# Layer 0's experts: the residual streams return from DRAM before the last pair's outputs, which one-hot products add on the chip

## The chip, the cores and the metric

One core of a Trainium2 chip runs the whole program. Its engines have a queue of instructions each: PE (TensorE matmuls, with PEld for the weight loads), DVE (VectorE), ACT (ScalarE), POOL (GpSimd) and SP (SyncE, which here only starts DMAs). The metric is the device time in microseconds (us). Three runs of the kernel before took 2985.73, 2987.39 and 2992.25 us.

## The reference

Two blocks of two layers each run one after the other on one stream of 512 tokens by 1024 features. The change lies in the first layer of the second block, which carries a second stream, a context of 256 tokens. At the end of that layer each stream gets the outputs of 16 experts, each expert picking its own tokens:

```python
def _expert_choice_ffn(h, w_router, w_gate, w_up, w_down):
    b, t, d = h.shape
    cap = EC_CAPACITY_FACTOR * t // N_EXPERTS          # 64 latent tokens, 32 context tokens
    aff = jax.nn.softmax(jnp.einsum('btd,de->bte', h, w_router).astype(jnp.float32), axis=-1)
    vals, idx = lax.top_k(aff.transpose(0, 2, 1), cap)
    xg = jax.vmap(lambda hb, ib: hb[ib])(h, idx)
    hid = jax.nn.silu(jnp.einsum('becd,edf->becf', xg, w_gate)) * jnp.einsum('becd,edf->becf', xg, w_up)
    out = jnp.einsum('becf,efd->becd', hid, w_down) * vals[..., None].astype(h.dtype)
    return jax.vmap(lambda ob, ib: jnp.zeros((t, d), h.dtype).at[ib.reshape(-1)].add(ob.reshape(-1, d)))(out, idx)

# in the layer:   x  = x  + m_lat[5] * _expert_choice_ffn(h2, ...)      (latent, 512 tokens)
#                 cx = cx + m_ctx[5] * _expert_choice_ffn(hc2, ...)     (context, 256 tokens)
# the next layer: h = rmsnorm(x) * ..., hc = rmsnorm(cx) * ...  and products with w_in
```

`rmsnorm` divides each token by the root of the mean of its 1024 squares. Everything is f32.

## The kernel before, in words

**The streams.** On the chip `x` (latent) and `cx` (context) lie with the features on the 128 partitions, as 8 slices of [128, tokens]. The router writes a copy with one token per row to DRAM, `acc`, and the experts' outputs are added there: row `r` of a tile `row` is added to the row of `acc` that an index names (`scatter`, L1811, an indirect DMA on POOL's queue that adds). After the last expert `reload` fetches `acc` back in six loads of 128 tokens (tile `in`, issued from ACT's queue, L1822), squares each token's row and sums it (ACT, L1824), turns it by 8 PE transposes (L1828) into PSUM, and DVE copies these into `x` and `cx` (L1830).

**The experts.** They are taken in eight pairs q = 0 to 7. For a pair, `gu` is the gate and up product: context experts on 32-column tiles of PE into PSUM tile `pso` (L1756), latent ones on 64-column tiles into `psg` (L1764). Four products with 32 columns, or two with 64, run side by side on PE; such a group is called a round below. Four transposes per stream turn the hidden rows (`hid`, L1738). `d` is the down product: context into `psa` (L1777), then latent in two halves of 512 features into `pss` (L1791). DVE scales each by the router's value and the layer's gate into `row` (L1783, L1794), and two scatters per stream add it to `acc`. The list `acts` in `ffn` sets the order: gu0, gu1, d0, gu2, d1, and so on to gu7, d6, d7.

**The weights** come in 96 pieces of 1 MB over SP's queue in the order of `acts`, into a ring of 14 slots: 11 of tile `ew` and 3 spare ones, which are the memory of `x` and `cx` themselves, since the streams are in DRAM meanwhile. The last pair's down product therefore still reads weights out of `x` (the rows `pss<-x,hid`).

**The scheduler** orders each engine's queue from its estimate of when inputs are there, so operations that are written one after the other in the code can be interleaved. PSUM has tags `g` (two tiles), `o`, `a`, `s` and `t`; a new tile waits until the readers of the old one are done.

**After the experts** the next layer's mixer norms both streams: the root from the sums (`rsqrt`, some ten DVE operations on a few columns, L309 to L325), one row of it over all partitions (`row_of`, L414 and L416), `norm_steps` (L439 to L449), and PE products with `w_in` whose weights are fetched and split by `load` (`wr`, `wh`, `wl`, L458 to L462; products L472 to L474). Where sums of squares are taken elsewhere in the kernel, PE multiplies the squares with a column of ones (L402).

Of the kernel before, what the change touches and what calls it, by code (L numbers as in the profile page):

```python
# [90 lines left out]
def _layout(inp):  # L91
# [16 lines left out]
    _layout2(g, A, vec2, c2)  # L108
    c2["id"] = np.eye(P, dtype=np.float32)
    A["const1"], coff = _pack(c)  # L110
    A["const2"], coff2 = _pack(c2)
# [123 lines left out]
class _K:  # L235
# [1324 lines left out]
    def route(self, l, v, x, nt, cap, state, got):  # L1560
# [61 lines left out]
        for r in range(ne):  # L1622
            o = pg[r * cap:(r + 1) * cap]
            ten.matmul(o[:, :ng], fi, one[:, r:16:ne], start=True, stop=False)
            ten.matmul(o[:, 8:16], val, one[:, r % 2:16:2], start=False, stop=r > 0)
            if r == 0:
                ten.matmul(o[:, 16:32], fi, one[:, :16], start=False, stop=True)
# [4 lines left out]
        vw = self.s1(f"vw{v}", [P, 8])  # L1632
        vec.tensor_copy(vw, pg[:, 8:16])
        yield

# [9 lines left out]
    def ffn(self, l, x, cx, need, states):  # L1645
        nc, A = self.nc, self.A
        ten, vec, act = nc.tensor, nc.vector, nc.scalar
        acts = [("gu", 0)] + [a for q in range(1, 8) for a in (("gu", q), ("d", q - 1))] + [("d", 7)]
        pieces = []
        for what, q in acts:  # L1650
# [9 lines left out]
        def fetch():  # L1660
            n = len(loaded) % (EW + len(spare))
            raw = self.tl("ew", [P, 4, 512]) if n < EW else spare[n - EW]
            nc.sync.dma_start(raw, pieces[len(loaded)].rearrange("p (k c) -> p k c", k=4))
            loaded.append(raw)
# [14 lines left out]
        for _ in range(6):  # L1679
            for r in run:  # L1680
                next(r, None)
        self.experts(l, acts, got, eload)
        if need:
            self.reload(x, cx)

# [20 lines left out]

    def experts(self, l, acts, got, eload):

# [3 lines left out]
        self.mods = {v: self.mod_cols(l, v, 3, self.v(f"n2{l}")) for v in got}  # L1712
        two = 1 in got
        rows, xg, hid = {}, {}, {}
# [53 lines left out]
        def down(q):  # L1768
            w = [[eload() for _ in range(2)] for _ in range(2)]
            if two:  # L1770
# [9 lines left out]
                for j in range(2):  # L1780
                    r = slice(j * 64, j * 64 + 64)
                    c = slice(j * 512, (j + 1) * 512)
                    vec.scalar_tensor_tensor(y[:64, c], ps[r], val[r, q:q + 1], gate[r, c], OP.mult, OP.mult)  # L1783
                self.scatter(1, y, si, q, 32)
            gi, si, val, gate = got[0]
            y = self.tl("row", [P, D])
            for j in range(2):
# [6 lines left out]
                vec.scalar_tensor_tensor(y[:, c], ps, val[:, q:q + 1], gate[:, c], OP.mult, OP.mult)  # L1794
            self.scatter(0, y, si, q, 64)

        fetch(0)
        fetch(1)
        inputs(0)
        for what, q in acts:  # L1800
            if what == "gu":
                fetch(q + 2)
                inputs(q + 1)
                gate_up(q)
            else:
                down(q)

# [7 lines left out]
    def reload(self, x, cx):  # L1815

        nc = self.nc
        ss = self.s1("ssr", [P, 6])
        for v, xs, nt, c0 in ((1, cx, 2, 0), (0, x, 4, 2)):
            for i in range(nt):  # L1820
                row = self.tl("in", [P, D])
                nc.scalar.dma_start(row, self.acc[v][i * P:(i + 1) * P, :])  # L1822
                j = self.tl("row", [P, D])
                nc.scalar.activation(j, row, AF.Square, accum_out=ss[:, c0 + i:c0 + i + 1])  # L1824
                for s in range(2):
                    pq = self.pt("t")
                    for k in range(4):
                        nc.tensor.transpose(pq[:, k * P:(k + 1) * P], row[:, (4 * s + k) * P:(4 * s + k + 1) * P], self.idf)  # L1828
                    d = xs[:, 4 * s:4 * s + 4, i * P:(i + 1) * P]
                    nc.vector.tensor_copy(d, pq.rearrange("p (k c) -> p k c", k=4))  # L1830
            c = slice(c0, c0 + nt)
            self.rsqrt(ss[:, c], nt, 1.0 / D, self.rs2[:, c])

# [58 lines left out]
```

## Time and profile before

| | |
|---|---|
| median of three runs | 2987.39 us (2985.73 to 2992.25) |
| the profiled execution | 2988.55 us, of which 2986.7 us are the span from the first to the last instruction |
| PE busy | 2787.1 us (93%) |
| DVE, ACT, POOL busy | 1544.5 us (52%), 1195.2 us (40%), 279.0 us (9%) |
| mean granted TensorE clock | 0.971 of 2.4 GHz |
| the experts of layer 0 whose order changes (gu7, d6, d7) | 2201.8 to 2253.3 us |
| return of the streams, to the latent root's start | 2253.3 to 2281.3 us |

A share of busy time is a mean over stages; what the change touches is the stretch of some 80 us from 2201.8 us on, some 3% of the span. There the rows further down are read: the windows give the busy time of each engine in a stretch, and the timeline gives the start and length of each instruction and what ended the idle time before it.

### The profile page before, as it was taken

The page shows a single profiled execution, that of the slowest core. Times are in us where ns is not written, and L with a number is a line of the kernel's source. Part 1 is how long each engine was busy: PE and PEld are TensorE (multiplying, and loading weights), DVE is VectorE, ACT ScalarE, POOL GpSimd, SP SyncE. Part 2 cuts the span into 40 slices and gives each one's busy share as a digit, 9 for nine tenths or more (in the row PEclk, how much of TensorE's full clock was granted, in tenths as well). Part 3 has the DMA queues.
Part 4 walks back from the last instruction along what each step waited for, and adds up shares of the span by engine and source line. Part 5 has one row for each costly group of instructions (what it writes and reads, how often), then busy time and mean ns, then how long its engine had stood idle before and what let it go on. Part 6 is the DMA issues. An engine that isn't in the chain of part 4 may idle for free. (4 is left out here: it accounts for less than half of the span.)

```text
span 2986.7 us, 46938 instructions
## 1 busy us (share of the span) xinstructions
PE 2787.1 (93%) x19055; PEld 1939.9 (65%) x19056; DVE 1544.5 (52%) x3135; ACT 1195.2 (40%) x2468; POOL 279.0 (9%) x276
## 2 busy tenths in 40 slices
PE   8999999999999999998999999899997999997875
PEld 6777767977777767977776878633324767773321
DVE  4645786545655786646356556711115465574100
ACT  5635354544645354444455243331113463533110
POOL 0000031000000030000011010011111010001101
PEclk9999999999999999999999999899997999998999
DMA  4142424412232424521100110689974111129997
GB/s 149 50 140 94 173 100 168 154 57 85 64 121 92 162 100 153 166 77 52 50 32 22 65 37 30 267 329 382 362 271 134 50 34 56 53 86 356 408 404 302
DMA packets 97576, 439.55 MB, mean 147 GB/s; under 512 B 11216, under 2 KB 12496, under 8 KB 72784
## 3 DMA queue, kind: packets, MB, share of 16 engines
q1 hardware_dynamic: 86976, 401.09, 36.4%
q0 software_dynamic: 9520, 32.32, 4.0%
q8 instruction: 150, 2.46, 0.3%
q10 hardware_dynamic: 864, 3.15, 0.3%
q14 instruction: 66, 0.54, 0.1%
HBM read 416.40 MB, written 20.97 MB: 146 GB/s over the span
## 5 line engine op out<-in xcount | busy, mean ns | idle before, releaser
L472 PE MATMUL psg<-h,wh 128*128 128x512 f32 x1616 | 653.9, 406 | 6.7 <-ACT h L444 4.3
L473 PE MATMUL psg<-h,wh 128*128 128x512 f32 x1616 | 649.8, 402 | 0.0
L474 PE MATMUL psg<-h,wl 128*128 128x512 f32 x1616 | 647.5, 401 | 1.2 <-DVE wl L462 0.7
L462 DVE TENSOR_TENSOR wl<-wr,wh 128x1024 fp32r<-128x1024 f32 (+2 forms) x272 | 338.9, 1247 | 351.9 <-ACT wh L460 348.5
L460 ACT ACTIVATE wh<-wr 128x1024 fp32r<-128x1024 f32 (+2 forms) x272 | 280.6, 1033 | 464.8 <-PE psg L473 387.3
L472 PEld LDWEIGHTS psg<-h,wh 128*128 128x128 f32 x1616 | 306.6, 190 | 90.4 <-issue 18.7
L474 PEld LDWEIGHTS psg<-h,wl 128*128 128x128 f32 x1616 | 306.4, 190 | 70.0 <-issue 7.8
L473 PEld LDWEIGHTS psg<-h,wh 128*128 128x128 f32 x1616 | 306.8, 190 | 68.2 <-issue 9.2
L1764 PE MATMUL psg<-ew,xg 128*64 128x512 f32 x832 | 222.6, 610 | 22.2 <-DMA ew<-in_eu_dram 12.2
L472 PE MATMUL psg<-y,wh 128*128 128x256 f32 (+1 forms) x560 | 180.5, 323 | 1.0 <-ACT y L448 0.3
L473 PE MATMUL psg<-y,wh 128*128 128x256 f32 (+1 forms) x560 | 179.2, 321 | 1.9 <-DVE y L449 1.9
L474 PE MATMUL psg<-y,wl 128*128 128x256 f32 (+1 forms) x560 | 178.6, 320 | 0.0
L1764 PEld LDWEIGHTS psg<-ew,xg 128*64 128x64 f32 x832 | 65.4, 139 | 154.6 <-issue 114.1
L472 PE MATMUL psg<-f,wh 128*128 128x256 f32 (+1 forms) x360 | 115.8, 323 | 6.0 <-DVE x L592 4.9
L472 PEld LDWEIGHTS psg<-y,wh 128*128 128x128 f32 x560 | 107.2, 192 | 15.1 <-issue 2.2
L1044 ACT ACTIVATE t<-pst 128x512 f32<-128x512 f32 (+1 forms) x134 | 69.7, 556 | 115.0 <-PE pst L1041 114.8
L473 PE MATMUL psg<-f,wh 128*128 128x256 f32 (+1 forms) x360 | 114.0, 317 | 0.7 <-DVE f L1279 0.7
L474 PE MATMUL psg<-f,wl 128*128 128x256 f32 (+1 forms) x360 | 113.8, 316 | 0.7 <-DVE wl L462 0.6
L473 PEld LDWEIGHTS psg<-y,wh 128*128 128x128 f32 x560 | 107.2, 192 | 10.7 <-DVE y L449 2.2
L474 PEld LDWEIGHTS psg<-y,wl 128*128 128x128 f32 x560 | 107.2, 192 | 6.4 <-issue 0.7
L1791 PE MATMUL pss<-ew,hid 128*64 128x512 f32 x400 | 106.5, 597 | 4.0 <-DMA ew<-in_ed_dram 4.0
L1041 PE MATMUL pst<-const_sb,t 128*128 128x128 f32 x488 | 85.9, 287 | 6.4 <-DVE t L1269 3.2
(484 smaller groups left out, 4589.8 us busy)
## 6 DMA issues: line engine op xcount, KB each, us to landing
ew<-in_eg_dram SPq DMA_DIRECT2D x52, 1024.0 KB, 9.3
ew<-in_eu_dram SPq DMA_DIRECT2D x52, 1024.0 KB, 20.9
ew<-in_ed_dram SPq DMA_DIRECT2D x50, 1024.0 KB, 9.5
wm<-in_wm_dram SPq DMA_DIRECT2D x96, 512.0 KB, 4.4
wr<-in_w_f_dram SPq DMA_DIRECT2D x92, 512.0 KB, 3.5
wr<-in_v_f_dram SPq DMA_DIRECT2D x60, 512.0 KB, 3.2
wr<-in_w_o_dram SPq DMA_DIRECT2D x32, 512.0 KB, 3.5
x<-in_ed_dram SPq DMA_DIRECT2D x10, 1024.0 KB, 22.0
```

The costliest lines, as they stand in the source:

```text
L460: nc.scalar.activation(hi, raw, AF.Copy)
L462: nc.vector.tensor_tensor(lo, raw, hi, OP.subtract)
L472: t.matmul(ps, a[0], b[0], start=first, stop=False)
L473: t.matmul(ps, a[0], b[1], start=False, stop=False)
L474: t.matmul(ps, a[1], b[0], start=False, stop=last)
L1041: ten.transpose(pp[:, (2 * i + a) * P:(2 * i + a + 1) * P], ps[a][:, c:c + P], self.idf)
L1044: self.nc.scalar.activation(pT[:, :w], pp[:, :w], AF.Copy)
L1764: ten.matmul(ps[e * 64:(e + 1) * 64], x0[:, d, e * 64:(e + 1) * 64], wn[e][:, k], start=d == 0, stop=d == 7)
L1791: ten.matmul(ps[e * 64:(e + 1) * 64], hid[0, q][:, f, e * 64:(e + 1) * 64], w[j][e][:, f], start=f == 0, stop=f == 3)
```

## The change

It applies to the layer with two streams only (`need`, `two`). The order of the last acts becomes gu6, d5, d6, gu7, d7, so that all weights that lie in `x` and `cx` are used up by d6; the last piece, the 96th, goes into an `ew` slot for the same reason. Pair 7 is not scattered. `reload` stands ahead of d7: its six loads go out from POOL's queue, and its squares and roots are gone. d7's rows are then added on the chip: `hot[v]` holds for each row of pair 7 a one at the token that it belongs to (made by comparing a row 0, 1, 2, ... with the token's number `ends`), and `add` multiplies the row with it (L1824 of after; 128x256 for the context, 128x512 for the latent stream, one per slice of 128 features), adds the product to `cx` or `x` on DVE (L1827), squares the sum on ACT (L1829), and sums the squares over features on PE (L1833). Two times four small products and two copies in `route` make `ends`.

```diff
@@ -1622,6 +1623,8 @@
         for r in range(ne):
             o = pg[r * cap:(r + 1) * cap]
             ten.matmul(o[:, :ng], fi, one[:, r:16:ne], start=True, stop=False)
+            if self.two and r < 2:
+                ten.matmul(o[:, 32:33], fi, one[:, 14 + r:15 + r], start=False, stop=False)
             ten.matmul(o[:, 8:16], val, one[:, r % 2:16:2], start=False, stop=r > 0)
             if r == 0:
                 ten.matmul(o[:, 16:32], fi, one[:, :16], start=False, stop=True)
@@ -1631,6 +1634,10 @@
         vec.tensor_copy(si, pg[:cap, 16:32])
         vw = self.s1(f"vw{v}", [P, 8])
         vec.tensor_copy(vw, pg[:, 8:16])
+        if self.two:
+
+            self.ends[v] = self.s1(f"ends{v}", [P, 1])[:2 * cap]
+            vec.tensor_copy(self.ends[v], pg[:2 * cap, 32:33])
         yield

         gate = self.s1(f"gate{v}", [P, D])
@@ -1646,6 +1653,9 @@
         nc, A = self.nc, self.A
         ten, vec, act = nc.tensor, nc.vector, nc.scalar
         acts = [("gu", 0)] + [a for q in range(1, 8) for a in (("gu", q), ("d", q - 1))] + [("d", 7)]
+        if need:
+            acts[-3:-1] = acts[-2], acts[-3]
+        self.two, self.ends = need, {}
         pieces = []
         for what, q in acts:
             ee = (2 * q, 2 * q + 1)
@@ -1659,7 +1669,8 @@

         def fetch():
             n = len(loaded) % (EW + len(spare))
-            raw = self.tl("ew", [P, 4, 512]) if n < EW else spare[n - EW]
+
+            raw = self.tl("ew", [P, 4, 512]) if n < EW or need and len(loaded) >= len(pieces) - 4 else spare[n - EW]
             nc.sync.dma_start(raw, pieces[len(loaded)].rearrange("p (k c) -> p k c", k=4))
             loaded.append(raw)

@@ -1679,9 +1690,7 @@
         for _ in range(6):
             for r in run:
                 next(r, None)
-        self.experts(l, acts, got, eload)
-        if need:
-            self.reload(x, cx)
+        self.experts(l, acts, got, eload, x, cx)

     def gather(self, v, gi, n):

@@ -1781,7 +1790,9 @@
                     r = slice(j * 64, j * 64 + 64)
                     c = slice(j * 512, (j + 1) * 512)
                     vec.scalar_tensor_tensor(y[:64, c], ps[r], val[r, q:q + 1], gate[r, c], OP.mult, OP.mult)
-                self.scatter(1, y, si, q, 32)
+                if q < 7:
+                    self.scatter(1, y, si, q, 32)
+                y1 = y
             gi, si, val, gate = got[0]
             y = self.tl("row", [P, D])
             for j in range(2):
@@ -1792,8 +1803,49 @@
                                    start=f == 0, stop=f == 3)
                 c = slice(j * 512, (j + 1) * 512)
                 vec.scalar_tensor_tensor(y[:, c], ps, val[:, q:q + 1], gate[:, c], OP.mult, OP.mult)
-            self.scatter(0, y, si, q, 64)
-
+                if two and q == 7:
+                    if j == 0:
+                        add(1, y1)
+                        scale(1)
+                    add(0, y, j)
+            if two and q == 7:
+                scale(0)
+            else:
+                self.scatter(0, y, si, q, 64)
+
+        def add(v, y, *halves):
+
+            w = 256 if v else 512
+            if v not in sums:
+                sums[v] = self.pt("ao"[v])[:, :2 if v else 4]
+            for k in range(0, KT, 2) if v else range(4 * halves[0], 4 * halves[0] + 4):
+                ps = self.pt("g")
+                for n in range(1 + v):
+                    ten.matmul(ps[:, n * w:n * w + w], y[:64 if v else P, (k + n) * P:(k + n + 1) * P], hot[v],
+                               start=True, stop=True)
+                d = (cx if v else x)[:, k:k + 1 + v]
+                vec.tensor_tensor(d, d, ps.rearrange("p (n c) -> p n c", n=1 + v), OP.add)
+                sq = self.tl("t", [P, 512])
+                act.activation(sq.rearrange("p (n c) -> p n c", n=1 + v), d, AF.Square)
+                nt = 2 if v else 4
+                for n in range(1 + v):
+                    for i in range(nt):
+                        ten.matmul(sums[v][:, i:i + 1], sq[:, n * w + i * P:n * w + (i + 1) * P], self.onesf[:, :1],
+                                   start=k + n + i == 0, stop=k + n == KT - 1 and i == nt - 1)
+
+        def scale(v):
+
+            nt = 2 if v else 4
+            self.rsqrt(sums[v], nt, 1.0 / D, self.rs2[:, 0:2] if v else self.rs2[:, 2:6])
+
+        if two:
+            io = self.tl("y", [P, 512])
+            nc.scalar.dma_start(io, self.A["iota"])
+            hot = {}
+            for v, w in ((0, 512), (1, 256)):
+                hot[v] = self.tl("y", [P, 512])[:(P, 64)[v], :w]
+                vec.tensor_scalar(hot[v], io[:(P, 64)[v], :w], self.ends[v], None, OP.is_equal)
+            sums = {}
         fetch(0)
         fetch(1)
         inputs(0)
@@ -1803,6 +1855,8 @@
                 inputs(q + 1)
                 gate_up(q)
             else:
+                if two and q == 7:
+                    self.reload(x, cx)
                 down(q)

     def scatter(self, v, y, si, q, n):
@@ -1815,21 +1869,16 @@
     def reload(self, x, cx):

         nc = self.nc
-        ss = self.s1("ssr", [P, 6])
-        for v, xs, nt, c0 in ((1, cx, 2, 0), (0, x, 4, 2)):
+        for v, xs, nt in ((1, cx, 2), (0, x, 4)):
             for i in range(nt):
                 row = self.tl("in", [P, D])
-                nc.scalar.dma_start(row, self.acc[v][i * P:(i + 1) * P, :])
-                j = self.tl("row", [P, D])
-                nc.scalar.activation(j, row, AF.Square, accum_out=ss[:, c0 + i:c0 + i + 1])
+                nc.gpsimd.dma_start(row, self.acc[v][i * P:(i + 1) * P, :])
                 for s in range(2):
                     pq = self.pt("t")
                     for k in range(4):
                         nc.tensor.transpose(pq[:, k * P:(k + 1) * P], row[:, (4 * s + k) * P:(4 * s + k + 1) * P], self.idf)
                     d = xs[:, 4 * s:4 * s + 4, i * P:(i + 1) * P]
                     nc.vector.tensor_copy(d, pq.rearrange("p (k c) -> p k c", k=4))
-            c = slice(c0, c0 + nt)
-            self.rsqrt(ss[:, c], nt, 1.0 / D, self.rs2[:, c])

     def block2(self, x, cx, rb, dram, out):
         self.rs2 = self.one("rs2", [P, 6])
```

On PE these are the rows from the end of d7 to the return of the streams in the kernel before (`pss` is d7's latent product, whose weights lie in `x`; `in` is a block of 128 tokens that came back, DMAHW the loads' semaphores):

```order
L1791 MATMUL pss_4122_20582<-ew_4117_20546,hid0_4105_20487 64x512
L1791 MATMUL pss_4122_20582<-x_72,hid0_4105_20487 64x512
L1828 MATMUL pst_4126_20599<-const2_sb_66,in_4124_20595 128x128 [waits DMAHW7_49]
L1828 MATMUL pst_4126_20599<-const2_sb_66,in_4124_20595 128x128 x3
L1828 MATMUL pst_4127_20605<-const2_sb_66,in_4124_20595 128x128 x4
L1828 MATMUL pst_4130_20615<-const2_sb_66,in_4128_20611 128x128 [waits DMAHW0_49,DVE_49]
L1828 MATMUL pst_4130_20615<-const2_sb_66,in_4128_20611 128x128 x3
L1828 MATMUL pst_4131_20621<-const2_sb_66,in_4128_20611 128x128 [waits DVE_49]
L1828 MATMUL pst_4131_20621<-const2_sb_66,in_4128_20611 128x128 x3
L1828 MATMUL pst_4142_20651<-const2_sb_66,in_4140_20647 128x128 [waits DMAHW1_49,DVE_49]
```

And these are the rows of the kernel after where d7 begins (L1747 the hidden transposes, L1786 and L1802 d7's context and latent products, L1879 the transposes of the blocks that came back, DMASW the semaphores of POOL's loads):

```order
L1747 MATMUL pst_4115_20522<-const2_sb_66,t_4113_20516 128x64 [waits DVE_49]
L1747 MATMUL pst_4115_20522<-const2_sb_66,t_4113_20516 128x64 x3
L1786 MATMUL psa_4142_20648<-ew_4138_20640,hid1_4116_20527 32x512 [waits DMAHW1_49,Activation_49]
L1747 MATMUL pst_4118_20549<-const2_sb_66,t_4117_20545 128x128 [waits DVE_49]
L1747 MATMUL pst_4118_20549<-const2_sb_66,t_4117_20545 128x128 x3
L1879 MATMUL pst_4121_20558<-const2_sb_66,in_4120_20556 128x128 [waits DMASW5_49,PE_49]
L1879 MATMUL pst_4121_20558<-const2_sb_66,in_4120_20556 128x128 x3
L1786 MATMUL psa_4142_20648<-ew_4139_20642,hid1_4116_20527 32x512 [waits DMAHW2_49]
L1879 MATMUL pst_4122_20564<-const2_sb_66,in_4120_20556 128x128 [waits Activation_49]
L1879 MATMUL pst_4122_20564<-const2_sb_66,in_4120_20556 128x128 x3
L1786 MATMUL psa_4142_20648<-ew_4140_20644,hid1_4116_20527 32x512 [waits DMAHW3_49]
L1802 MATMUL pss_4145_20669<-ew_4138_20640,hid0_4119_20554 64x512
```

The transposes stood behind the whole of d7 and waited for six loads; now they stand between d7's products, and every switch goes from one tile shape of PE to another.

Behind d7's last products PE's queue of the kernel after ends the experts with these rows (L415 is `row_of` for the context; L1824 the one-hot products, `y` the one-hot tile; L1833 the sums of squares):

```order
L415 MATMUL pst_4199_20917<-const2_sb_66,rs2_13280 128x128 [waits DVE_49]
L415 MATMUL pst_4199_20917<-const2_sb_66,rs2_13280 128x128
L1824 MATMUL psg_4173_20787<-y_3892_19113,row_4144_20668 128x512 [waits DVE_49]
L1824 MATMUL psg_4175_20796<-y_3892_19113,row_4144_20668 128x512 [waits PE_49]
L1824 MATMUL psg_4177_20805<-y_3892_19113,row_4144_20668 128x512 [waits DVE_49]
L1833 MATMUL psa_4163_20740<-onesf_70,t_4174_20790 128x1 [waits Activation_49]
L1833 MATMUL psa_4163_20740<-onesf_70,t_4174_20790 128x1 x3
L1824 MATMUL psg_4179_20814<-y_3892_19113,row_4144_20668 128x512 [waits DVE_49]
L1833 MATMUL psa_4163_20740<-onesf_70,t_4176_20799 128x1 [waits Activation_49]
L1833 MATMUL psa_4163_20740<-onesf_70,t_4176_20799 128x1 x3
L1833 MATMUL psa_4163_20740<-onesf_70,t_4178_20808 128x1 [waits Activation_49]
L1833 MATMUL psa_4163_20740<-onesf_70,t_4178_20808 128x1 x3
```

Nothing like this stands in the kernel before: the last four of the latent stream's eight one-hot products and all their sums come behind d7, the rest stands between d7's products. Each product waits for DVE (the row, or the PSUM tile that the add before it frees) and each sum for ACT's square. Only then can the latent root start.

POOL's queue of the kernel before ends the experts with these rows (`si` are the token numbers; `row_4119` and `row_4120` are pair 7's outputs; the last row is the next layer's load of a mask):

```order
L1811 DMA acc0256_18745<-row_4119_20566,si1_3877_19065 256x1024 [waits DMASW4_49,DVE_49]
L1811 DMA acc0512_18744<-row_4120_20571,si0_3872_19047 512x1024 [waits DMASW5_49,DVE_49]
L1811 DMA acc0256_18745<-row_4119_20566,si1_3877_19065 256x1024 [waits DMASW6_49]
L1811 DMA acc0512_18744<-row_4120_20571,si0_3872_19047 512x1024 [waits DMASW7_49]
L1174 DMA f3_4244_21122<-in_namask_dram 128x1024 [waits DMAHW5_49,DMAHW3_49,DMAHW7_49,DMAHW1_49,PE_49]
```

and that of the kernel after with these (L1865 the scatters of pair 6, L1875 the loads of the return):

```order
L1865 DMA acc0256_18745<-row_4098_20421,si1_3878_19071 256x1024 [waits DMASW7_49,DVE_49]
L1865 DMA acc0256_18745<-row_4098_20421,si1_3878_19071 256x1024 [waits DMASW2_49]
L1865 DMA acc0512_18744<-row_4099_20426,si0_3872_19049 512x1024 [waits DMASW1_49,DVE_49]
L1875 DMA in_4120_20556<-acc0256_18745 128x1024 [waits DMASW3_49,PE_49]
L1875 DMA in_4123_20570<-acc0256_18745 128x1024 [waits PE_49]
L1865 DMA acc0512_18744<-row_4099_20426,si0_3872_19049 512x1024 [waits DMASW4_49]
L1875 DMA in_4126_20584<-acc0512_18744 128x1024 [waits DMASW7_49,PE_49]
L1875 DMA in_4129_20598<-acc0512_18744 128x1024 [waits PE_49]
L1875 DMA in_4132_20612<-acc0512_18744 128x1024 [waits DMASW5_49,PE_49]
L1875 DMA in_4135_20626<-acc0512_18744 128x1024 [waits DMASW6_49,PE_49]
L1175 DMA f3_4269_21234<-in_namask_dram 128x1024 [waits DMAHW4_49,DMAHW3_49,DMAHW6_49,DMAHW2_49,DMAHW0_49]
```

The four scatters of pair 7 are gone, and the six loads have moved from ACT's queue to POOL's, behind or between pair 6's scatters; `in` loads also wait until PE has read the tile that lay there.

## Rows read from the trace of the kernel before

**Rows 1.** the page: span, busy times, and PE's clock in 40 slices

```profile
span 2986.7 us, 46938 instructions
...
PE 2787.1 (93%) x19055; PEld 1939.9 (65%) x19056; DVE 1544.5 (52%) x3135; ACT 1195.2 (40%) x2468; POOL 279.0 (9%) x276
...
PEclk9999999999999999999999999899997999998999
```

**Rows 2.** windows: us, busy PE, PEld, DVE, ACT, POOL, PEclk, DMA, GB/s

```profile
2220.00:2240.00 20.00, 20.00 (x96) 5.78 (x94) 4.80 (x8) 2.17 (x4) 1.31 (x1) 1.00 0.05 8
2240.00:2260.00 20.00, 13.36 (x64) 3.33 (x60) 3.48 (x5) 0.00 (x0) 8.16 (x6) 0.89 0.60 125
2260.00:2280.00 20.00, 10.48 (x45) 8.36 (x45) 8.58 (x22) 6.79 (x12) 3.23 (x3) 0.51 0.71 217
2280.00:2300.00 20.00, 15.32 (x76) 12.98 (x76) 18.36 (x48) 10.44 (x19) 0.00 (x0) 0.74 0.32 106
```

**Rows 3.** timeline: gu7, d6, d7 begin; d7's last products

```profile
2201.83 0.62 PE L1756 MATMUL pso<-ew,xg 128*32 128x512 f32 x1
...
2225.51 1.05 PE L1777 MATMUL psa<-ew,hid 128*32 128x512 f32 x2
...
2239.62 1.05 PE L1777 MATMUL psa<-ew,hid 128*32 128x512 f32 x4
...
2252.34 1.02 PE L1791 MATMUL pss<-x,hid 128*64 128x512 f32 x2
```

**Rows 4.** timeline: from the last scatter to the latent root

```profile
2261.79 1.40 POOL L1811 DMA_INDIRECT acc<-row,si  x1 [4.34 <-DMA f<-in_cos_dram]
2262.20 6.97 ACTq L1822 DMA_DIRECT2D in<-acc  x3
...
2265.93 1.97 PE L1828 MATMUL pst<-const_sb,in 128*128 128x128 f32 x8 [12.57 <-DMA in<-acc]
...
2275.37 5.28 PE L1828 MATMUL pst<-const_sb,in 128*128 128x128 f32 x24 [1.38 <-DVE rq_t L322]
...
2279.25 2.14 DVE L1830 COPY x<-pst 128x512 f32<-128x512 f32 x3 [0.16 <-PE pst L1828]
...
2281.30 0.16 DVE L309 TENSOR_SCALAR rq_a<-ssr 128x4 f32<-128x4 f32 x1
```

**Rows 5.** timeline: two rounds of gu7; transposes, and sums, at full clock

```profile
2205.88 0.59 PE L1764 MATMUL psg<-ew,xg 128*64 128x512 f32 x1
...
2206.31 0.59 PE L1764 MATMUL psg<-ew,xg 128*64 128x512 f32 x1
...
1957.59 0.66 PE L1701 MATMUL pst<-const_sb,in 128*128 128x128 f32 x4
...
1916.33 1.05 PE L402 MATMUL pst<-onesf,y 128*128 128x1 f32 x8
```

**Rows 6.** timeline: two neighbouring products of the next mixer

```profile
2316.84 0.40 PE L474 MATMUL psg<-h,wl 128*128 128x512 f32 x1
2317.07 0.40 PE L472 MATMUL psg<-h,wh 128*128 128x512 f32 x1
```

**Rows 7.** DMA issues: queue, count, KB each, median us to landing

```profile
acc<-in POOLq DMA_DIRECT2D x6, 512.0 KB, 11.5
...
in<-acc ACTq DMA_DIRECT2D x6, 512.0 KB, 5.6
```

**Rows 8.** windows of 2 us, columns as in rows 2

```profile
2252.00:2254.00 2.00, 1.36 (x6) 0.19 (x2) 0.72 (x2) 0.00 (x0) 0.93 (x1) 1.00 0.34 41
2256.00:2258.00 2.00, 0.00 (x0) 0.00 (x0) 0.00 (x0) 0.00 (x0) 1.32 (x1) 0.50 1.08 274
...
1922.00:1924.00 2.00, 2.00 (x11) 1.55 (x10) 0.73 (x4) 2.00 (x4) 1.12 (x2) 0.50 0.10 43
```

**Rows 9.** timeline: a scatter during gu7; the next mixer's first latent norm

```profile
2211.53 1.40 POOL L1811 DMA_INDIRECT acc<-row,si  x1 [7.13 <-DMA acc<-row,si]
...
2291.66 0.74 DVE L439 SCALAR_TENSOR_TENSOR t<-x,mA,t 128x512 f32<-128x512 f32 x1
```

More of the change, by code (lines that the diff above doesn't have):

```diff
@@ L109, in _layout @@
     c2["id"] = np.eye(P, dtype=np.float32)
+    A["iota"] = _bc(np.arange(T, dtype=np.float32))
     A["const1"], coff = _pack(c)
@@ L1705, in modulated, with experts @@
         return o
-    def experts(self, l, acts, got, eload):
+    def experts(self, l, acts, got, eload, x, cx):
         nc = self.nc
@@ L1712, in experts @@
         self.mods = {v: self.mod_cols(l, v, 3, self.v(f"n2{l}")) for v in got}
-        two = 1 in got
+        two = self.two
         rows, xg, hid = {}, {}, {}
```

## The prediction

> **What bounds the kernel now.** I read the page first. PE is busy 93% of the span at a mean granted clock of 0.971, DVE 52% [rows 1]; so time is lost mainly where PE waits, and a stage that leaves PE later moves all PE work behind it by as much. Then the windows of 20 us around the change [rows 2]: PE is full to 2240, has 13.4 us of 20 and then 10.5 of 20 at clock 0.51, and 15.3 of 20 in the stretch to 2300. The reader is to see that no other engine is full there either (POOL 8.2, DVE 8.6): this is a chain of waits. The timeline gives its links. gu7 begins at 2201.83, d6 at 2225.51, d7 at 2239.62, and d7 ends at 2252.34 + 1.02 = 2253.4 [rows 3]. The last scatter is issued at 2261.79 after 4.34 us of idling, the reload's loads from 2262.20; the first transposes start at 2265.93 after 12.57 us in which PE did nothing; the last 24 begin at 2275.37; the latent root starts at 2281.30 [rows 4]. So from d7's end to the root 27.9 us pass.
>
> **The change, part by part.**
>
> *Units.* An f32 product of 512 columns makes two passes, and passes start 2206.31 − 2205.88 = 0.43 us apart [rows 5]; two 64-column or four 32-column products share them. A full-width 128x512 product therefore costs 0.86, a 128x256 one 0.43. Four transposes take 0.66 with the end of the last, 0.14 each in a row; the eight records of 1.05 us are four 128x1 sums (two passes each), 0.23 a sum when the last record's own end is taken off [rows 5].
>
> *The order gu7, d6, d7 becomes d6, gu7, d7.* d6 is 24 passes, 10.3 us, and took 14.1 because its rows are broken up by waits for weight pieces; before gu7 the pieces have all come, and the order shows its products paired throughout: 10.6. gu7 took 23.7 [rows 3] for 52 passes (22.4); in the new order its context and latent rows stand mixed and make 58: 24.9 and 1.0 of waits, 25.9. d7 then starts at T = 2201.8 + 10.6 + 25.9 = 2238.3, against 2239.6: **−1.3**. If gu7 stays as before, −3.5; if d6 stays at 14.1, +2.2.
>
> *Removed behind d7:* the four scatters of pair 7, the load behind them, ACT's squares and the wait of 12.57 us. Of the 27.9 us the 48 transposes stay, at full clock 48 × 0.14 = 6.7 (12 DVE copies beside them). That removes **21.2**.
>
> *Is the return hidden?* d6's scatters now run under gu7, where a scatter waits up to 7.13 us for the one before it [rows 9]; four of them in two chains from about 2213 end by 2228 to 2231. The loads wait for them on POOL's queue and land 5.6 us later at the old reload's median, 11.5 at that of POOL's plain stores [rows 7]. DMA is free there (share 0.05 in 2220 to 2240, rows 2). I take 5.6, the same direction and addresses: the first four are on the chip by about 2242, the last two must wait for an `in` tile that d7's first transposes free, and land at T + 10.5 and T + 13.5, while PE comes to them at T + 13.4 and T + 15.6. So they cost nothing; without that cover see case D.
>
> *Added on PE:* 8 one-hot products of 256 columns, 3.4, and 8 of 512, 6.9: **10.3**; 48 sums, **11.0**. Together 21.3, and the whole of it lies between d7's start and the latent root, on the engine whose end sets the root. This is the core of the forecast: the waits that go, 21.2, are replaced by PE work of 21.3. Bounds for the products: the mixer's rounded f32 products of 512 columns start 0.23 apart [rows 6], which gives 2.8 for all of them; but `row` and the one-hot tile are plain f32, as the expert tiles are, so I take 10.3 and keep 2.8 for the range. The sums cannot be below half of 11.0 if each took one pass.
>
> *Switches and chain.* d7's passes go from 30 to 34, since transposes break its pairs (14.6 against 13.7): **+0.9**. Some 25 changes between tile shapes, about 0.1 each, an estimate from what gu7 takes above its 52 passes now (23.7 − 22.4 = 1.3 for a dozen changes): **+2.5**. At the end, slices 4 to 7 of the latent stream run: scaling 0.75, product 0.86, add 0.75, square some 0.7, sums 0.9; with two PSUM tiles for the product PE waits about **+3** in all. DVE has 12 adds more, 9 us, beside PE's 49.
>
> *Routing* gets four tiny products, two copies, a 256 KB load on ACT's queue and two compares of a few tenths on DVE, while the gather of rows waits for a store anyway: 0 to 0.5, I take **+0.3**.
>
> *Behind the root* both kernels do the same: root, row, then DVE-bound norms, with the first latent norm at 2291.66 [rows 9], 10.4 us after the root's start. The weights are there in both.
>
> Sum, at d7's end plus return: PE from T needs 14.6 + 6.7 + 10.3 + 11.0 + 1.1 (gu7's hidden transposes) + 0.4 (context row) + 2.5 + 2.6 ≈ 49.2, the root starts at 2238.3 + 49.2 = 2287.5, against 2281.3: **+6.2**; with the routing **+6.5**. The other way: −1.3 − 21.2 + 21.3 + 0.9 + 2.5 + 3 + 0.3 = +5.5, and hidden transposes that d7's start used to include +1.1: the same within rounding. The profiled execution is 2988.55, so 2995.0; the median of the runs is 1.2 lower, and so is the forecast: **2994**.
>
> **The rivals.**
>
> *B, not slower: the one-hot products run at the rate of rows 6.* Then 7.5 us go out of the sum and it ends at −1.0: 2986.5. The point is 6.5 us: the sum crosses zero if products and sums together take 14.8 instead of 21.3. For it speaks only that they have no tile split, against it that full-width f32 transposes (128 columns, 0.14) already cost two passes' worth, as 512 columns at 0.86 do: 0.86/4 = 0.21 is nearer than 0.06.
>
> *C, slower still: the clock falls while the outputs are added.* The trace shows granted clock 1.00 at d7's end, and 0.50 (1.2 GHz) in the window behind, where PE did nothing; but it also shows 0.50 at 1922 to 1924 with PE busy for the whole 2.00 us, in the router's chain of small products and waits [rows 8]. The last 26 us before the root are such a chain. At 1.2 GHz for half of it +13, for all +26: about 3007 and 3020. Against it: the sums of rows 5 ran at full clock with short waits between them. The Trainium skill, "TensorE: Matmul & The Clock Gate", section "A second HAM failure mode: psum-queue depth-cycling", says that micro-idles between groups of products, as banks are cycled, make the clock swing between half and full; this kernel cycles two PSUM tiles in that way. By that rule C would be the likely case, by the rows it is one in seven.
>
> *D: the return comes late.* POOL's queue holds scatter, load, load, scatter, then four loads, so a late scatter holds all. If the last two loads take 11.5 instead of 5.6 [rows 7] d7's second half and the latent adds stand still for 4 to 9 us: 2999 to 3003. The Trainium skill, "SBUF — State Buffer", section "SBUF: two separate sides", warns that DMAs from GpSimd's queue starve while DVE runs a copy between SBUF tensors on both ports, since their descriptors can't be written. Here DVE's copies read PSUM, and no row shows such a starvation; by that rule the return would come in D's time.
>
> *E: no gain or loss at all.* The part removed and the part added are within 0.1 us of each other, so that E is A with the small terms (6 us) hidden by each other.
>
> **How the numbers follow.** This kernel's runs tell 0.2% (6.0 us: 2981.4 and 2993.4) from no change. A (with E), 2994, own range 2989 to 2999: 0.57, of it slower 0.30, same 0.24, faster 0.03. B, 2986.5: 0.20, of it same 0.13, faster 0.07. C, 3000 to 3020: 0.15, D, 2999 to 3003: 0.08, both slower. Faster 0.10, same 0.37, slower 0.53. The range goes from below B, if gu7 keeps its 23.7 too (2984), to C's half (3006).
>
> **What the changed profile would show.** gu7 behind d6, d6 in about 10.6 us and d7 beginning near 2238; loads of `in` on POOL's queue issued before 2240 and no idle time of PE over 2 us for them. Products L1824 starting 0.86 apart (512 columns) and sums in groups of 4 taking about 1.05; the latent root starting near 2287.5; from there the old distance of 10.4 us to the first latent norm, and equal stages behind. Wrong would be: one-hot products 0.23 apart (B); granted clock near 0.5 between d7's middle and the root (C); PE waiting for DMA `in` inside d7 (D). It would also be wrong if the sums overlapped the products, or if the mixer behind took up the shift.

## The result: slower by 0.58%, and the profile after

Six runs of the changed kernel took 2998.50 to 3009.88 us, median 3007.15; six of the kernel before, beside them, 2985.73 to 2992.25, median 2987.43. The ratio is 1.0058, 95% interval 1.0048 to 1.0068: some 17 us more, while the medians differ by 19.7. The forecast was 2994, 6.5 us more, with a range to 3006. The direction was right, the size not: the median lies just above the range, and 1.0058 times the median before, 3004.8, just inside it. That the range reaches so far is owed to its rival C, whose half it was to end at (3007 by C's own sum), and not to the sum of the forecast: that it nearly holds the time is no success of that sum.

The page of the changed kernel (the profiled execution took 3005.45 us; the lines answer to [rows 1]):

```profile
span 3003.7 us, 47237 instructions
...
PE 2814.9 (94%) x19192; PEld 1957.6 (65%) x19192; DVE 1552.9 (52%) x3151; ACT 1195.2 (40%) x2468; POOL 276.9 (9%) x278
...
PEclk9999999999999999998999999899997999998998
```

PE is busy 27.8 us more, the span is 17.0 us longer. The windows of 20 us (columns as in [rows 2]: length, busy PE, PEld, DVE, ACT, POOL, then PE's clock, DMA share, GB/s):

```profile
2240.00:2260.00 20.00, 20.00 (x109) 9.20 (x108) 11.29 (x17) 1.23 (x2) 2.74 (x4) 1.00 0.33 104
2260.00:2280.00 20.00, 20.00 (x71) 12.92 (x69) 5.96 (x19) 4.42 (x7) 0.00 (x0) 0.63 0.00 1
2280.00:2300.00 20.00, 17.29 (x73) 10.33 (x72) 5.87 (x22) 2.91 (x5) 0.00 (x0) 0.76 0.15 53
2300.00:2320.00 20.00, 17.43 (x83) 14.81 (x83) 18.17 (x34) 11.88 (x21) 0.00 (x0) 0.77 0.32 105
```

In [rows 2] PE stood idle for much of the first three stretches. Now it is full in the first two, 20.00 of 20.00, and the clock falls all the same: 1.00 in the first, 0.63 in the second, 0.76 in the third. Being busy and being fast are two columns. The timeline gives the links (d6's first product, gu7's first, the first hidden transposes, d7's first product, the last load of the return, its last transposes, then sums and products, last the latent root's start):

```profile
2201.34 0.62 PE L1786 MATMUL psa<-ew,hid 128*32 128x512 f32 x1
...
2211.93 1.06 PE L1765 MATMUL pso<-ew,xg 128*32 128x512 f32 x6
...
2238.16 0.46 PE L1747 MATMUL pst<-const_sb,t 64*128 64x64 f32 x4
2239.09 1.04 PE L1786 MATMUL psa<-ew,hid 128*32 128x512 f32 x2 [0.47 <-ACT hid L1749]
...
2246.03 0.53 POOL L1875 DMA_DIRECT2D in<-acc  x1 [2.47 <-PE pst L1879]
...
2252.72 1.09 PE L1879 MATMUL pst<-const_sb,in 128*128 128x128 f32 x8
...
2262.60 1.05 PE L1833 MATMUL pso<-onesf,t 128*128 128x1 f32 x8
...
2266.18 1.71 PE L1833 MATMUL pso<-onesf,t 128*128 128x1 f32 x8
2267.75 2.05 PE L1824 MATMUL psg<-y,row 128*128 128x512 f32 x2
...
2297.32 0.16 DVE L310 TENSOR_SCALAR rq_a<-psa 128x4 f32<-128x4 f32 x1 [1.89 <-PE psa L1833]
```

No PE row of the return has a wait for a DMA. Four such sums take 1.05 us at 2262.60 and 1.71 at 2266.18. From the start of this part of the program (gu7's first product at 2201.83 before, d6's at 2201.34 after) to the latent root it was 79.5 us before [rows 3, 4] and is 96.0 now: +16.5 of the span's +17.0. Everything behind moved with it.

In windows of 2 us the clock is 1.00 up to 2264, 0.75 in the next, 0.50 in the eleven windows from 2266 to 2288, 0.77 in one more, then 1.00. The two at either end:

```profile
2264.00:2266.00 2.00, 2.00 (x6) 0.92 (x5) 0.69 (x1) 0.66 (x2) 0.00 (x0) 0.75 0.00 0
2266.00:2268.00 2.00, 2.00 (x10) 1.81 (x9) 0.69 (x1) 0.73 (x2) 0.00 (x0) 0.50 0.00 0
...
2286.00:2288.00 2.00, 2.00 (x5) 0.46 (x2) 0.00 (x0) 0.00 (x0) 0.00 (x0) 0.50 0.00 0
2288.00:2290.00 2.00, 1.52 (x5) 0.26 (x3) 0.75 (x1) 0.38 (x1) 0.00 (x0) 0.77 0.00 0
```

At half clock PE does half the work, so this costs 0.5 + 11 × 1.0 + 0.46 = 12.0 us. Without it the root would lie 84.0 us behind d6's start, an estimate; the forecast said 2287.5 − 2201.8 = 85.7. So the suspicion is plain from one trace: the forecast's sum of work holds, and the clock (its case C) came on top. The kernel before has a low stretch as long, 0.50 in the eleven windows of 2 us from 2256 to 2278, but PE is busy for only 8.5 of those 22 us; what is new is that PE is full while the clock is low. The mean clock doesn't show it: 0.971 before, 0.973 now. But a low clock can also be a symptom. The experiments take the work and the clock apart.

### The profile page after: what moved, and what is told of

Its sections match the earlier page's. It is cut to its first block, busy times and chain, and to the rows that moved or that the text cites. A ratio compares the mean times of both kernels' runs of the same rounds, so it can differ in the third digit from the quotient of the medians.

```text
span 3003.7 us, 47237 instructions
## 1 busy us (share of the span) xinstructions
PE 2814.9 (94%) x19192; PEld 1957.6 (65%) x19192; DVE 1552.9 (52%) x3151; ACT 1195.2 (40%) x2468; POOL 276.9 (9%) x278
## 5 line engine op out<-in xcount | busy, mean ns | idle before, releaser
L1802 PE MATMUL pss<-ew,hid 128*64 128x512 f32 x384 | 107.6, 614 | 2.6 <-DMA ew<-in_ed_dram 2.6
```

What stands on the lines that cost most here:

```text
L1802: ten.matmul(ps[e * 64:(e + 1) * 64], hid[0, q][:, f, e * 64:(e + 1) * 64], w[j][e][:, f], start=f == 0, stop=f == 3)
```

## The experiments

In the order of the runs; "the root" is always the time from d6's first product to the latent root's start in the profiled execution. Each was timed beside the kernel before, whose medians in the four sessions were 2987.7 to 2988.9 us. The profiled executions also differ elsewhere: the part behind the root took 701.1 to 709.4 us in them. So whole times are compared by the medians and ratios of many runs, and the stretch by the root.

**The same work as dense products.**

```diff
-                    for i in range(nt):
-                        ten.matmul(sums[v][:, i:i + 1], sq[:, n * w + i * P:n * w + (i + 1) * P], self.onesf[:, :1], ...)
+                    ten.matmul(sums[v], self.onesf, sq[:, n * w:n * w + w], start=k + n == 0, stop=k + n == KT - 1)
```

(Not shown: in `scale` ACT copies one row of the sums, and tiny products turn it into columns.)

> The 48 sums of 128x1 become 12 f32 products of the squares with a full tile of ones (8 of 512 columns, 4 pairs of 256, two passes each: 10.3 us of PE instead of 11.0), and a copied row and a few tiny products turn the sums into columns (about 2 us on the chain). PE's work is the same. Theory C (the granted clock falls to 0.50 for 23.5 us because this stretch is made of small, waiting operations, and half of that, 11.7 us, is the loss): the clock stays at 1.00 through the adds and the time falls by about 10, to some 2995. Rival W (the loss is the amount of work put in, and the clock falls whatever the sums look like): 3005 to 3007.

Measured: 2997.19 us (2995.32 to 3002.68), ratio 1.0029 (1.0019 to 1.0038), 10.0 less than the changed kernel by the medians, 8.7 by the ratios. The root: 88.3 us, 7.7 less. Windows of 6 us, first of the changed kernel, then of this one:

```profile
2262.00:2268.00 6.00, 6.00 (x26) 4.36 (x26) 2.06 (x3) 1.89 (x3) 0.00 (x0) 0.75 0.00 0
2268.00:2274.00 6.00, 6.00 (x18) 3.93 (x18) 1.83 (x6) 0.63 (x1) 0.00 (x0) 0.50 0.00 0
2280.00:2286.00 6.00, 6.00 (x24) 4.11 (x24) 0.00 (x0) 0.00 (x0) 0.00 (x0) 0.50 0.00 0
```

```profile
2262.00:2268.00 6.00, 6.00 (x23) 3.92 (x23) 1.97 (x4) 1.89 (x3) 0.00 (x0) 1.00 0.01 3
2268.00:2274.00 6.00, 6.00 (x20) 3.12 (x19) 3.19 (x15) 2.16 (x4) 0.00 (x0) 1.00 0.00 0
2280.00:2286.00 6.00, 5.28 (x12) 2.22 (x13) 2.72 (x4) 1.89 (x3) 0.00 (x0) 1.00 0.25 87
```

PE is no busier than in the changed kernel, in the last row it even waits, and the clock is 1.00 up to the root. C gave 2995, W 3005 to 3007: W is out. That the root is not at 84.0 but at 88.3 is at least in part the longer chain: behind d7 PE waits 0.84 us for the last row, 1.44 for the last square and 0.68 for the copied row, against 0.48 in all in the changed kernel.

**Fewer sums.**

```diff
-                nt = 2 if v else 4
-                for n in range(1 + v):
-                    for i in range(nt):
-                        ten.matmul(sums[v][:, i:i + 1], sq[...], self.onesf[:, :1], ...)
+                if not first and not last:
+                    vec.tensor_tensor(acc[v], acc[v], sq, OP.add)
+                if last:
+                    cols = [c[...] for c in (acc[v], sq) for n in range(1 + v) for i in range(nt)]
+                    for m, c in enumerate(cols):
+                        ten.matmul(sums[v][:, m % nt:m % nt + 1], c, self.onesf[:, :1], ...)
```

(Shortened: `...` stands for arguments and slices; `acc[v]` is a tile that the first slice's squares are written to.)

> DVE adds the squares of a stream's slices together and PE sums only the total and the last slice: 16 sums instead of 48, 7.4 us of PE less, 9 adds of some 0.7 us more on DVE, which is idle most of this stretch. W: 7 to 8 us less than the changed kernel, 2997. C: the clock stays up as well, or falls for a shorter time, and the time comes down by 13 to 19, to 2986 to 2992.

Measured: 2987.92 us (2984.43 to 2994.43), ratio 1.0005 (0.9995 to 1.0016): 19.2 less than the changed kernel by the medians, 15.8 by the ratios. The clock is 1.00 in every window up to the root, which comes 16.8 us earlier. Of these the clock is 12.0; the other 4.8 are the 32 sums left out (7.4 by the forecast's unit) less new waits, 1.72 us of them for DVE's last addition of squares. C's range held. Four of its products, and its root (d6 began at 2200.38, so 79.2 us):

```profile
2271.74 3.89 PE L1824 MATMUL psg<-y,row 128*128 128x512 f32 x8 [0.85 <-DVE row L1805]
...
2279.55 0.16 DVE L310 TENSOR_SCALAR rq_a<-psa 128x4 f32<-128x4 f32 x1 [2.04 <-PE psa L1840]
```

Eight records are four products: 0.97 each with the waits between them, 0.86 without by the forecast, not the 0.23 of rival B.

**More dense work.**

```diff
-                    ten.matmul(ps[:, n * w:n * w + w], y[...], hot[v], start=True, stop=True)
+                    for _ in range(2):
+                        ten.matmul(ps[:, n * w:n * w + w], y[...], hot[v], start=True, stop=True)
```

> Each one-hot product is made twice into the same PSUM tile: 10.3 us more of PE work at full clock, all of it dense products. W: the work adds up, 10 to 20 us more than the changed kernel, 3015 to 3025. C: the dense products keep the clock up and its 11.7 us are saved, so that the time stays where it is, 3000 to 3007, with granted clock 1.00 in the stretch.

Measured: 3010.37 us (3010.25 to 3010.85, four runs), ratio 1.0073 (1.0052 to 1.0094). 10.3 us of work were added, and the median went up by 3.2. W's 3015 to 3025 missed by 5 us, C's 3000 to 3007 by 3; and C had the clock at 1.00 throughout, but it fell, for a shorter time.

```profile
2262.00:2268.00 6.00, 6.00 (x23) 4.78 (x23) 1.18 (x2) 1.26 (x2) 0.00 (x0) 0.57 0.00 0
2268.00:2274.00 6.00, 6.00 (x14) 3.57 (x15) 1.29 (x6) 0.63 (x1) 0.00 (x0) 0.50 0.00 0
2274.00:2280.00 6.00, 6.00 (x24) 3.47 (x23) 2.42 (x10) 0.63 (x1) 0.00 (x0) 0.80 0.00 0
```

It is back at 1.00 from 2278 on, counted from d6's start some ten us earlier than in the changed kernel. Its low windows up to the root cost 6.8 us, its root lies at 101.9: 101.9 − 6.8 = 95.1, against 84.0 for the changed kernel without its low clock. The difference is 11.1, about the 10.3 that were put in.

**The order alone**: the kernel before with `acts[-3:-1] = acts[-2], acts[-3]` for the first layer and nothing else.

> The kernel before with nothing but the new order gu6, d5, d6, gu7, d7. By the forecast's term d7 starts 1.3 us earlier (d6 unbroken at 10.6 us, gu7 longer by 2.2) and everything behind it moves with it: 2986, not to be told from the kernel before. If the swap itself cost the time (a wait for weights in gu7, a later scatter), it would be slower by some us, 2990 to 2995.

Measured: 2989.90 us (2985.60 to 2996.22), ratio 1.0007 (0.9995 to 1.0018); no difference that can be told. The root 80.2 us against 79.5. d7 begins 37.7 us behind the start of d6 in this kernel and in the changed one, just as it began 37.8 us behind that of gu7 before [rows 3]; the forecast had 36.5, without the hidden transposes ahead of d7. The waits stay where they were, though pair 6's scatters are long done:

```profile
2263.26 1.40 POOL L1813 DMA_INDIRECT acc<-row,si  x1 [3.61 <-DMA f<-in_cos_dram]
...
2267.61 1.94 PE L1830 MATMUL pst<-const_sb,in 128*128 128x128 f32 x8 [12.05 <-DMA in<-acc]
```

12.05 us of PE's waiting instead of 12.57 [rows 4]: it is pair 7's own scatters that hold the return.

**Cheaper products**, on top of the fewer sums: first with rows split into a rounded part and its rest, then with rounded rows alone.

```diff
-                    ten.matmul(ps[...], y[...], hot[v], start=True, stop=True)
+                    ten.matmul(ps[...], y[0][:, c], hot[v], start=True, stop=False)
+                    ten.matmul(ps[...], y[1][:, c], hot[v], start=False, stop=True)
```

> On top of the accumulated squares (2987.9): pair 7's rows are split into a rounded part and its rest, and each one-hot product becomes two products of rounded operands. By rival B's rows these start 0.23 us apart for 512 columns and 0.12 for 256, so the products take 5.6 us instead of 10.3; the split puts an ACT copy and a DVE subtraction (some 1.4 us) ahead of the last half. If the clock stays at 1.00, 2 to 4 us less, 2984 to 2986. If the clock falls again because less dense work is left between the waits, 2990 to 2995.

```diff
-            y = self.tl("row", [P, D])
+            y = self.tl("row", [P, D], *([F32R] if two and q == 7 else []))
-                hot[v] = self.tl("y", [P, 512])[:(P, 64)[v], :w]
+                hot[v] = self.tl("y", [P, 512], F32R)[:(P, 64)[v], :w]
```

> On top of the accumulated squares (2987.9): DVE writes pair 7's rows rounded, the one-hot tile likewise, and a product is one pass as in rival B: 2.8 us instead of 10.3. The rest of the rows' value is left out. If PE bounds this stretch, 7 us less, 2981; if DVE's chain of adds and squares takes over (12 adds, 10 additions of squares and 4 scalings of 0.7 us, 18 us), 3 to 5 less, 2983 to 2985. If the clock falls, 2988 or more.

(Not shown: the lines that split the rows.) Measured: 2990.54 us (ratio 1.0012, 1.0003 to 1.0022) and 2990.36 (0.9999, 0.9989 to 1.0009). Neither can be told from the fewer sums with f32 products (2987.92, 1.0005). These are the times that both expectations gave for a falling clock. The rounded rows alone, windows of 6 us:

```profile
2268.00:2274.00 6.00, 4.18 (x21) 2.45 (x20) 3.15 (x12) 1.89 (x3) 0.00 (x0) 0.79 0.24 87
2274.00:2280.00 6.00, 3.34 (x6) 1.37 (x6) 5.78 (x16) 2.62 (x5) 0.00 (x0) 0.50 0.00 0
2280.00:2286.00 6.00, 3.57 (x16) 3.49 (x16) 2.13 (x11) 0.81 (x2) 0.00 (x0) 0.50 0.04 8
```

PE's work went down, DVE is full in the middle (5.78 of 6), PE waits, and the clock is at 0.50 ahead of the root, where it was 1.00 with f32 products: it falls with 16 narrow sums too. The last sums, at the end of the path, then run at half speed. How much of the missing gain is DVE's chain and how much the clock, these two runs don't separate; the profiled roots are 80.7 and 78.8 us.

**Two other orders, and the squares added on POOL**: the first two each on top of the fewer sums, the third on top of the second.

```diff
-                    self.reload(x, cx)
+                    loaded = self.reload(x, cx)
...
                     if j == 0:
+                        self.turn(loaded)
                         add(1, y1)
```

> On top of the accumulated squares (2987.9): the loads of the return go out as before, the context's into tiles of their own, but the transposes stand in the code behind the first half of d7's latent product, so that d7's products are paired again and the transposes fill the waits of the one-hot chain. d7 is 4 to 6 passes shorter and one or two waits of 0.8 us on PE are filled: 2 to 4 us less, 2984 to 2986. If the transposes now delay the adds, no gain, 2988.

```diff
-                if two and q == 7:
-                    if j == 0:
-                        add(1, y1)
-                        scale(1)
-                    add(0, y, j)
             if two and q == 7:
+                add(1, y1)
+                scale(1)
+                add(0, y, 0)
+                add(0, y, 1)
                 scale(0)
```

> On top of the accumulated squares (2987.9): the adds stand in the code behind both halves of d7's latent product, so that PE finishes d7 first and the one-hot products follow each other without the wait of some 0.9 us for the second half's scaling in the middle. PE's work is the same; DVE (12 adds, 9 additions of squares, 4 scalings, 0.7 us each, 17 us) has all of it behind d7 and would bound the chain: the root 2 to 4 us earlier, 2984 to 2986. If the clock falls in the longer run of waiting products, 2988 to 2995.

```diff
-                    vec.tensor_tensor(acc[v], acc[v], sq, OP.add)
+                    pool.tensor_tensor(acc[v], acc[v], sq, OP.add)
```

> The same with the additions of squares on POOL (some 1.1 us each, beside DVE): DVE's part of the chain is 11 us, and PE's products (10.3) bound it nearly. The root 4 to 6 us earlier than with the accumulated squares alone, 2982 to 2984. If POOL's adds, one after the other, are the new end of the chain, no better than with DVE, 2985 to 2988. If the clock falls, more.

Measured: 2990.70 us (1.0005, 0.9995 to 1.0014), 2987.91 (1.0002, 0.9993 to 1.0011) and 2989.97 (1.0011, 1.0002 to 1.0020). None of the expected 2 to 6 us came. PE's wait in the middle is gone in the second, but each latent slice then takes an add and an addition of squares on DVE, 0.68 us each, and PE waits for DVE about 0.2 us before each of the last three products and 1.80 before the last sums; POOL in DVE's place was no quicker. In all three the clock also falls at the last eight sums or just ahead of them, so that they take 3.5 to 3.7 us of PE instead of 2.1. With the fewer sums alone it falls too, but just behind the root (0.80 in 2280 to 2282); from one trace of each it can't be told whether that is more than luck. None of these three beats the kernel before.

**Without the products**: on top of the fewer sums, the lines of the 16 products and 12 adds are deleted, so that pair 7's outputs are left out of both streams.

> The accumulated squares without the 16 one-hot products and their 12 adds: pair 7's outputs are left out of both streams, the squares and sums stay. By the forecast's terms 10.3 us of PE and the waits for the adds (2 to 3) go from the path to the latent root: 2975 to 2977. If the products hide beside DVE's chain, or the clock falls when they are gone, 2980 to 2985.

Measured: 2976.87 us (2975.68 to 2981.11), ratio 0.9962 (0.9949 to 0.9976): 11.0 less than with them, the root 67.1 instead of 79.2. That is the price of the products on the path, 10.3 by the forecast plus 1 to 2 of waits, and rather more, since the clock fell to 0.62 in 2268 to 2270 and the last four sums took 1.84 us. It is also about the most that a cheaper addition could give in this order.

**Forty-eight sums in two bunches**, on top of the fewer sums: each sum is made three times, and the scale is divided by three (not shown).

```diff
-                    cols = [c[...] for c in (acc[v], sq) for n in range(1 + v) for i in range(nt)]
+                    cols = [c[...] for c in 3 * (acc[v], sq) for n in range(1 + v) for i in range(nt)]
```

> The accumulated squares, but each of the 16 sums of 128x1 is made three times and the scale divided by three: 48 sums as in the changed kernel, 11.0 us of PE, in two bunches of 24 (one per stream) instead of one group of four between every two products. If only the amount counts (W), 7.4 us more than the accumulated squares, 2995, at clock 1.00. If narrow sums lower the clock wherever they stand (C), the clock falls during or behind the first bunch and the latent products behind it run at 1.2 GHz: 3000 to 3008, as in the changed kernel. If it is the alternation of single products and sums that lowers it, the clock holds through the products and 2995 comes out as with W.

Measured: 3004.10 us (3002.64 to 3006.00), ratio 1.0050 (1.0034 to 1.0067). The root is 11.8 us later than with the fewer sums (91.0 to 79.2). Of these 7.4 are the 32 sums more, which W has as well; the rest is the clock, whose low windows up to the root cost some 5 us. The time is in C's range, and W's 2995 is 9 us off. The first bunch on PE, eight records (four sums) a row, and windows of 2 us:

```profile
2266.37 0.95 PE L1840 MATMUL pso<-onesf,y 128*128 128x1 f32 x8
2267.18 1.03 PE L1840 MATMUL pso<-onesf,t 128*128 128x1 f32 x8
2268.08 1.03 PE L1840 MATMUL pso<-onesf,y 128*128 128x1 f32 x8
2268.97 1.03 PE L1840 MATMUL pso<-onesf,t 128*128 128x1 f32 x8
2269.86 1.55 PE L1840 MATMUL pso<-onesf,y 128*128 128x1 f32 x8
2271.27 1.84 PE L1840 MATMUL pso<-onesf,t 128*128 128x1 f32 x8
2272.98 4.83 PE L1824 MATMUL psg<-y,row 128*128 128x512 f32 x6
```

```profile
2268.00:2270.00 2.00, 2.00 (x20) 2.00 (x20) 0.00 (x0) 0.00 (x0) 0.00 (x0) 1.00 0.00 0
2270.00:2272.00 2.00, 2.00 (x13) 2.00 (x12) 0.00 (x0) 0.00 (x0) 0.00 (x0) 0.55 0.00 0
2272.00:2274.00 2.00, 2.00 (x8) 1.48 (x8) 0.53 (x4) 0.00 (x0) 0.00 (x0) 0.50 0.00 0
```

They follow each other with no idle time before any of them, and in the middle of the bunch the granted clock drops from 1.00 to 0.50; during the products and the latent passes behind it, it comes back (0.74 in 2276 to 2278, then 1.00). In the second bunch it falls again. PEld, the weight load, is as full as PE: every sum loads 128 columns of squares as weights, for one column of ones that moves. No run separates the two.

## Why the prediction fell short

**The sum of work was nearly right.** Return of the streams: no wait of PE for it, the loads on POOL's queue landed in 3.9 us at the median (the forecast took 5.6, case D 11.5), and the last of them was issued at 2246.03, in good time for its transposes. The 48 transposes took 6.7 us of PE, as forecast. The waits are gone from PE's row. Products: 11.0 us by leaving them out (12.1 by the root), against 10.3 and waits. Sums: the changed kernel's own are 1.05 us for four at full clock. Behind the root nothing changed (14.9 us to the first latent product against 14.6).

**Small terms.** The forecast's T is where gu7 ends and the hidden transposes begin: 36.5 us behind the start, and measured 2238.16 − 2201.34 = 36.8 (d6 10.6, as said, gu7 26.2 instead of 25.9). Its −1.3 sets this T against a start of d7 that includes hidden transposes; with the 1.1 that the sum adds for them the order was forecast at −0.2, and it is 0. From T to the root 59.2 us pass, 47.2 without the 12.0 of the clock, instead of 49.2: the guesses for switches and closing chain were too large by 2. Here the 12.0 is an estimate too: at full clock PE might have waited longer for DVE and ACT than its 0.48 us behind d7, as the dense sums and the fewer sums show (3.0 and 2.6). Together the forecast's root is 1.7 us too late, before the clock.

**The step that failed** is the weighing of case C: "Against it: the sums of rows 5 ran at full clock with short waits between them", and "by the rows it is one in seven". Four sums at full clock say nothing about what follows when there are 48. The forecast had counted 11.0 us of sums as work like any other, at full clock. The row that it took for C, 1922 to 1924 [rows 8], doesn't show a busy PE losing its clock: PE had waited 2.32 us just before, and the clock fell then:

```profile
1920.00:1922.00 2.00, 0.31 (x2) 0.31 (x3) 1.68 (x13) 1.53 (x4) 0.00 (x0) 0.81 0.00 0
...
1921.69 1.12 PE L1598 MATMUL pss<-const_sb,x 128*128 128x128 f32 x4 [2.32 <-ACT in L1600]
```

The trace of the kernel before has the right row some 45 us earlier: thirteen products of 16 columns (26 records), one behind the other, and then the clock falls to 0.50 under dense products, with PE busy in every window:

```profile
1872.93 2.97 PE L1540 MATMUL pst<-y,mB 128*128 128x16 f32 x26
...
1874.00:1876.00 2.00, 2.00 (x20) 2.00 (x20) 0.51 (x2) 0.00 (x0) 0.00 (x0) 1.00 0.00 0
1876.00:1878.00 2.00, 2.00 (x11) 1.66 (x11) 1.22 (x4) 0.63 (x1) 0.00 (x0) 0.72 0.00 0
1878.00:1880.00 2.00, 2.00 (x6) 1.61 (x5) 1.29 (x4) 0.00 (x0) 0.00 (x0) 0.50 0.45 101
```

The price in C was right, +13 for half of the stretch: 12.0 was lost in the profiled execution, and 3007 was C's time for it. Its reason, a chain of small products and waits, was right in the small products and not in the waits.

Shown by runs: that the narrow sums bring the clock down (dense sums: 1.00 and 10 us less; fewer sums: 1.00 and 19 less; 48 in bunches without waits: down again), and that the work alone doesn't explain the time. By the Trainium skill, "TensorE: Matmul & The Clock Gate", section "A second HAM failure mode: psum-queue depth-cycling", short idle times between groups of products, as PSUM tiles are cycled, make the clock swing between half and full. The clock did fall here, but the cycling by itself isn't the cause: the dense sums cycle the same two PSUM tiles at 1.00, and the bunched sums, which cycle none, fall to 0.50. Nor do the profiles show idle time of PE there (2.00 of 2.00 us); since they model where a product ends, a gap hidden in its record isn't excluded.

**B** is out by the products' rows and by their price. **The gain that the change was to bring** is there: the wait of 12.57 us and the waits between the transposes behind it are off the path. It is spent again on the same engine, 10.3 for products and 11.0 for sums, and then some by the clock. With 32 of the sums moved to DVE the account is even, 2987.9 to 2988.2 in the same session.

What stays open: why the cheaper products and the better orders gave nothing beyond the fewer sums. Their traces show DVE's chain and a clock that falls ahead of the root, but no run holds the one fixed and changes the other. Open too is what else brings the clock down there, with 16 narrow sums and with waits of PE.

## What to carry to other kernels

Price a wait that is removed against the work that replaces it on the engine that ends the stage; here 21 us of waiting were paid for with 21 us of PE. A reduction by many 128x1 products can cost more than its records say, by what happens to the clock of the products around it (here 11.0 us of sums and 12.0 of clock): add the squares up on an idle engine first, or make the sums dense. And read PE's clock beside its busy time, since a stage can be 100% busy at half speed.

## What was not expected of the hardware

Back-to-back 128x1 products halved the granted clock (1.00 to 0.50, four sums going from 1.03 to 1.84 us) while PE was busy without a gap. In the six runs of the changed kernel the time goes with the clock: the fastest, 2998.50 us, had a mean granted clock of 0.976, the three slowest, 3008.85 to 3009.88, had 0.970; 0.006 of 3000 us is 18 us of clock, against a spread of 11. It is no rule: of the runs with fewer sums one took 2993.17 us at 0.976 and another 2987.49 at 0.973.
